# FFN gate and up by seven products of halves for half of each column group, and the FFN in five stretches

## The chip, the cores and the metric

The kernel runs on one core of a Trainium2 chip, as one program. The metric is the device time of one execution in microseconds (us), as the median of several runs. A core has five engines that run side by side and wait for each other by semaphores: TensorE (PE, matrix products; its weight loads are shown as PEld), VectorE (DVE), ScalarE (ACT), GpSimd (POOL) and SyncE (SP, which here issues all DMAs). Matmuls accumulate in PSUM, eight banks of 512 fp32 values per partition; everything else lies in SBUF.

## The reference

A decoder trunk of two layers over 256 tokens of width 2048, all in fp32. Layer A mixes by a gated position mixing beside attention to a memory, layer B by latent attention beside attention to a memory. Each layer then has a dense SwiGLU FFN with a hidden width of 5632:

```
def swiglu_ffn(h, w_gate, w_up, w_down):
    return (jax.nn.silu(h @ w_gate) * (h @ w_up)) @ w_down
...
    h = h + rms_norm(mix, norm_gains[i, 1])
    f = swiglu_ffn(rms_norm(h, norm_gains[i, 2]), ffn_w_gate[i], ffn_w_up[i], ffn_w_down[i])
    h = h + rms_norm(f, norm_gains[i, 3])
```

The change concerns `h @ w_gate` and `h @ w_up`, two products of 256 x 2048 by 2048 x 5632 per layer.

## The kernel before

**Numbers.** Every large product is done in three matmuls (`mm3`, L208 to L214): each operand is split into a rounded high half (`hi`) and the rest (`lo`), and hi x hi, hi x lo and lo x hi are added up in PSUM. ScalarE makes `hi`, VectorE makes `lo` as source minus `hi`. `wsplit` (L174 to L188) does it for 1024 weight values per partition at a time; with a gain, both operations also multiply each contraction row by its norm gain, so that the features themselves can stay unscaled. `split` (L164) does it for features.

**FFN stages.** `ffn` (L404) works in stretches of groups. A group is 512 gate and 512 up columns, and a stretch takes 3, 4 and then 4 groups (`parts`). For each group `stream` (L190) loads 1 MB of weights per DMA, two contraction tiles of 128 rows, and yields them split. `tok_major` (L223) runs 12 matmuls 512 wide on each tile: two token halves, gate and up, three matmuls. After 16 tiles the four banks hold gate and up of both token halves. ScalarE then applies Silu with the row's norm factor `r` (L427), VectorE multiplies it with up (L429), four transposes per token half turn the result into features (`turn`, L236, transposes at L240), and these are split into the pair `hp`.

After a stretch `to_tokens` multiplies `hp` with the rows of `w_down` that belong to it. The first stretch leaves its result in `Y` (L445), the second adds to it (L447), and the last runs through `residual`, which ends the layer.

**Buffers.** Weights are staged in three buffers `wst` of two tiles each, and split into a ring of four `whi` and four `wlo`. The eight PSUM banks form two sets of four, which groups take in turn; while one set is summed up, the other is read out, and its banks also take the transposes (`short`).

**Order.** The small work beside the matmuls is written as generators in a list `bg`, and `tick` advances them after each contraction tile. The framework that builds the program then sets the order of each engine's queue anew, by the order of the text and by when it expects operands to be ready; `issue_after` pins a few of them. On the chip each engine runs its queue in that order, and an instruction that waits holds up all behind it on that engine.

**Norm.** `norm_scale` (L247) computes the norm factor of each token, as a column `r_x` for token-major results, and (if `R` is given) as a row `R_x` over all partitions by one more small matmul (L268).

Of the kernel before, what the change touches and what calls it, by code (L numbers as in the profile page):

```python
# [17 lines left out]
P = 128  # L18
D = 2048
# [29 lines left out]
def trunk(ctx, tc, x, mem, positions, norm_gains, w_mem_kv, w_down, a_w_in, a_b_s, a_w_out, w_kv_a, w_uk, w_uv,  # L49
# [199 lines left out]
    def norm_scale(src, r, R):  # L249

        ss = sm.tile([P, 2, 4], F32, tag="ss", name="ss")
        for b in range(2):
            for j in range(4):
                with behind(line["act"]):
                    sumsq(src[b][:, j * 512:(j + 1) * 512], ss[:, b, j:j + 1])
                if j % 2:
                    yield
        s1 = sm.tile([P, 2], F32, tag="s2", name="s2")
        dve.tensor_reduce(out=s1, in_=ss, axis=AX.X, op=ALU.add)
        rstd(r, mean_eps(s1, 2, 1.0 / D), 2)  # L260
        if R is None:
            return
# [140 lines left out]

    def ffn(i, xp, r, gcol, gb, each, hp, need):  # L404
        parts = [(0, 3), (3, 4), (7, 4)]
        behind_group = []

        def to_features(hvs, f):

            for b in range(2):  # L410
                turn(hvs[b], hp, b, f)
                yield

        for pi, (c0, ncn) in enumerate(parts):
            for c in range(ncn):
                X = g4()
                col = (c0 + c) * 1024
                for k, wt, first, last in stream([w_gate_up[i]], [(col, 1024)], list(range(KD)), gcol):
                    tok_major(xp, k, wt, 0, 512, [X[:2], X[2:]], first, last)
                    tick()  # L420
                if pi == 0 and c == 0:
                    drain([need])
                drain(behind_group)
                hvs = []
                for b in range(2):
                    sg = tmp.tile([P, 512], F32, tag="sg", name="sg")
                    act.activation(out=sg, in_=X[2 * b], func=AF.Silu, scale=r[:, b:b + 1])  # L427
                    hv = tmp.tile([P, 512], F32, tag="hv", name="hv")
                    dve.scalar_tensor_tensor(out=hv, in0=X[2 * b + 1], scalar=r[:, b:b + 1], in1=sg,  # L429
                                             op0=ALU.mult, op1=ALU.mult)  # L430
                    hvs.append(hv)
                short["banks"] = X
                behind_group[:] = [to_features(hvs, c * 4)]
                bg.append(behind_group[0])
            ks = list(range(ncn * 4))
# [5 lines left out]
            if pi < len(parts) - 1:  # L441
                def evac(b, c, n, o):
                    yv = Y[:, b, c:c + n]
                    if pi == 0:
                        act.copy(out=yv, in_=o)  # L445
                    else:
                        dve.tensor_tensor(out=yv, in0=o, in1=yv, op=ALU.add)  # L447

                to_tokens(w_down[i], hp, ks, c0 * 4, evac, gate=gate)
            else:  # L450
                return to_tokens(w_down[i], hp, ks, c0 * 4, *residual(gb, False, each, i == 0), gate=gate)

# [35 lines left out]
    for i in range(2):  # L488
        kT = const.tile([P, 4, S], F32, name=f"mk{i}")
        vm = const.tile([P, 2, 512], F32, name=f"mv{i}")  # L490
        X = g4()
# [70 lines left out]
    with tc.tile_pool(name="mixa", bufs=1) as ma:  # L562
# [4 lines left out]
                             compare_op=ALU.is_ge, fill=0.0)  # L567
        bs = ma.tile([P, NH, P], F32, name="bs")
        sp.dma_start(out=bs, in_=a_b_s.broadcast_to([P, NH, P]))
# [142 lines left out]

    need = chain(rest, norm_scale([h[:, b, :] for b in range(2)], r_x, None))
    bg += [need, tables()]
    rest = ffn(0, xp, r_x, G_F0, gain_bcast(0, 3), turned(pair_b), pair_a, need)


    bg.append(chain(rest, norm_scale([h[:, b, :] for b in range(2)], r_x, R_x)))
    xp, mp = pair_b, pair_a
    qT = mb.tile([P, 4, S], F32, name="qTb")  # L720
    L = g4()
# [43 lines left out]
    drain([lat])  # L765
    krT = [mb.tile([P, S], F32, name=f"krT{e}") for e in range(2)]

    def rope(dst, src, n):
# [4 lines left out]
        for lo, c1, c2, op in ((0, cb, sb, ALU.subtract), (32, sb, cb, ALU.add)):  # L773
            t1 = mb.tile([P, 2, 4, 32], F32, tag="rope1", name="rope1")[:, :, :n, :]
            t2 = mb.tile([P, 2, 4, 32], F32, tag="rope2", name="rope2")[:, :, :n, :]
            dve.tensor_tensor(out=t1, in0=x1, in1=c1, op=ALU.mult)
# [116 lines left out]
    for g in lat:  # L893
        next(g)
    short["banks"] = [M[3], L[2], L[3]]
    bg[:0] = lat
# [29 lines left out]

    need = chain(rest, norm_scale([h[:, b, :] for b in range(2)], r_x, None))
    bg.append(need)
    ffn(1, xp, r_x, G_F1, gain_bcast(1, 3), store, pair_a, need)

# [41 lines left out]
```

## Time and profile before

| | |
|---|---|
| median of 3 runs | 2157.45 us (2156.25 to 2158.76) |
| profiled execution, its own time | 2159.11 us |
| its span | 2157.4 us |
| TensorE busy | 99% of the span, 10670 matmuls |
| weight loads (PEld) | 84%, beside the matmuls |
| VectorE busy | 55%, 1527 instructions |
| ScalarE busy | 47%, 1248 instructions |
| DMA | 398.71 MB, 54.9% of the 16 engines' time |

The span is the time from the first to the last instruction of one profiled execution. TensorE's durations in the rows overlap, since a matmul starts while the one before is still draining; what one costs is read from the distance between starts. In section 2 of the page the span is cut into 40 slices, and each digit is a busy share in tenths.

### The profile page before, as it was taken

Reading aid. Unit: us, or ns where it says so; the run is one execution under the profiler, and the core shown is the slowest. Engines: PE = TensorE matmul, PEld = TensorE weight load, DVE = VectorE, ACT = ScalarE, POOL = GpSimd, SP = SyncE. Lnnn points to the kernel's source line nnn. Section 1 sums busy time; section 2 is a strip of 40 time slices with the busy share of each in tenths; the row PEclk is TensorE's granted clock in tenths of the full one; section 3 lists DMA queues with packets and bytes.
Section 4 is the critical chain, followed back from the end, with each engine's and each line's share of the span. In section 5 each row is a group of like instructions: output and inputs, shape, how many; then the busy total and the mean of one; then the engine's idle time right before and its main releaser. Section 6 shows DMA issues by size and latency. Waiting matters only on the chain.

```text
span 2157.4 us, 26321 instructions
## 1 busy us (share of the span) xinstructions
PE 2134.8 (99%) x10670; PEld 1802.1 (84%) x10670; DVE 1191.9 (55%) x1527; ACT 1014.5 (47%) x1248; POOL 4.8 (0%) x11
## 2 busy tenths in 40 slices
PE   8999999999999999999999999999999999999998
PEld 7889989788888888888899998978888888888888
DVE  6556576644444454444467775664444445444456
ACT  6545445544444443444455654554444444344443
POOL 0000000000000000000000000000000000000000
PEclk9999999999999999999999999999999999999999
DMA  9655365555555555555553544555555555555554
GB/s 365 251 176 173 121 215 195 192 178 190 182 192 178 190 180 195 177 192 178 175 195 134 185 132 137 176 195 176 191 182 192 178 191 179 195 177 193 177 175 137
DMA packets 115849, 398.71 MB, mean 185 GB/s; under 512 B 7184, under 2 KB 15632, under 8 KB 114704
## 3 DMA queue, kind: packets, MB, share of 16 engines
q1 hardware_dynamic: 115728, 397.04, 54.9%
q8 instruction: 83, 1.36, 0.2%
q14 instruction: 38, 0.31, 0.0%
HBM read 394.91 MB, written 2.10 MB: 184 GB/s over the span
## 4 chain that ended last, share of the span: by engine, by line
PE 96%; DVE 3%; ACT 1%; issue 0%; DMA 0%; SPq 0%; DVEq 0%; ACTq 0%
PE bank L213 31%; PE bank L214 31%; PE bank L212 31%; PE bank L240 1%; DVE wlo L187 1%; DVE h L364 0%; PE bank L857 0%; PE bank L858 0%; PE bank L550 0%; PE bank L882 0%; ACT whi L185 0%; PE bank L604 0%; DVE hl L167 0%; PE bank L544 0%; ACT hl L166 0%
## 5 line engine op out<-in xcount | busy, mean ns | idle before, releaser
L212 PE MATMUL bank<-whi,hl 128*128 128x512 f32 (+3 forms) x2752 | 1057.7, 385 | 0.8 <-ACT hl L166 0.7
L213 PE MATMUL bank<-wlo,hl 128*128 128x512 f32 (+3 forms) x2752 | 1051.9, 382 | 1.9 <-DVE wlo L187 1.5
L214 PE MATMUL bank<-whi,hl 128*128 128x512 f32 (+3 forms) x2752 | 1051.6, 382 | 0.0
L187 DVE SCALAR_TENSOR_TENSOR wlo<-wst,gains,whi 128x1024 fp32r<-128x1024 f32 (+3 forms) x504 | 625.9, 1245 | 586.2 <-ACT whi L185 583.5
L185 ACT ACTIVATE whi<-wst,gains 128x1024 fp32r<-128x1024 f32 (+3 forms) x504 | 564.5, 1122 | 681.9 <-PE bank L214 569.6
L213 PEld LDWEIGHTS bank<-wlo,hl 128*128 128x128 f32 x2752 | 517.5, 188 | 103.4 <-DVE wlo L187 2.8
L214 PEld LDWEIGHTS bank<-whi,hl 128*128 128x128 f32 x2752 | 517.0, 188 | 104.0 <-DVE hl L167 0.4
L212 PEld LDWEIGHTS bank<-whi,hl 128*128 128x128 f32 x2752 | 517.2, 188 | 100.6 <-ACT hl L166 1.5
L181 DVE TENSOR_TENSOR wlo<-wst,whi 128x1024 fp32r<-128x1024 f32 (+1 forms) x256 | 296.1, 1157 | 313.4 <-ACT whi L179 313.3
L179 ACT CAST whi<-wst 128x1024 fp32r<-128x1024 f32 (+1 forms) x256 | 254.5, 995 | 362.6 <-PE bank L214 340.7
L212 PE MATMUL bank<-hl,whi 128*128 128x256 f32 x448 | 129.1, 288 | 6.7 <-ACT whi L185 6.7
L214 PE MATMUL bank<-hl,wlo 128*128 128x256 f32 x448 | 127.0, 284 | 1.2 <-DVE wlo L187 1.2
L213 PE MATMUL bank<-hl,whi 128*128 128x256 f32 x448 | 127.0, 284 | 0.0
L212 PEld LDWEIGHTS bank<-hl,whi 128*128 128x128 f32 x448 | 85.1, 190 | 9.9 <-ACT whi L185 6.7
L213 PEld LDWEIGHTS bank<-hl,whi 128*128 128x128 f32 x448 | 85.1, 190 | 2.7
L214 PEld LDWEIGHTS bank<-hl,wlo 128*128 128x128 f32 x448 | 84.8, 190 | 1.7 <-DVE wlo L187 1.6
L167 DVE TENSOR_TENSOR hl<-bank,hl 128x512 fp32r<-128x512 f32 (+2 forms) x97 | 55.2, 580 | 1.3 <-ACT hl L166 0.6
L166 ACT CAST hl<-bank 128x512 fp32r<-128x512 f32 (+2 forms) x97 | 46.7, 493 | 12.4 <-PE bank L240 8.7
L427 ACT ACTIVATE sg<-bank,r_x 128x512 f32<-128x512 f32 x44 | 29.7, 680 | 8.1 <-PE bank L214 8.1
L429 DVE SCALAR_TENSOR_TENSOR hv<-bank,r_x,sg 128x512 f32<-128x512 f32 x44 | 30.9, 745 | 1.4 <-ACT sg L427 1.4
L212 PE MATMUL bank<-cT,whi 128*128 128x256 f32 x96 | 28.1, 293 | 0.0
L213 PE MATMUL bank<-cT,whi 128*128 128x256 f32 x96 | 27.5, 287 | 0.0
(172 smaller groups left out, 742.4 us busy)
## 6 DMA issues: line engine op xcount, KB each, us to landing
wst<-in_w_gate_up SPq DMA_DIRECT2D x176, 1024.0 KB, 4.9
wst<-in_ffn_w_down SPq DMA_DIRECT2D x72, 1024.0 KB, 4.8
wst<-in_a_w_in SPq DMA_DIRECT2D x24, 1024.0 KB, 5.1
wst<-in_w_mem_kv SPq DMA_DIRECT2D x15, 1024.0 KB, 6.9
wst<-in_ffn_w_down SPq DMA_DIRECT2D x16, 768.0 KB, 4.3
wst<-in_a_w_out SPq DMA_DIRECT2D x8, 1024.0 KB, 4.8
wst<-in_b_w_in SPq DMA_DIRECT2D x8, 1024.0 KB, 5.0
wst<-in_b_w_out SPq DMA_DIRECT2D x8, 1024.0 KB, 5.4
```

What stands on the lines that cost most here:

```text
L166: ins = act.copy(out=hi, in_=src)
L167: dve.tensor_tensor(out=lo, in0=src, in1=hi.bitcast(F32), op=ALU.subtract)
L179: act.copy(out=hi[:, :n], in_=src)
L181: dve.tensor_tensor(out=lo[:, :n], in0=src, in1=hi[:, :n].bitcast(F32), op=ALU.subtract)
L185: act.activation(out=hi[:, :n], in_=src, func=AF.Copy, scale=g)
L187: dve.scalar_tensor_tensor(out=lo[:, :n], in0=src, scalar=g, in1=hi[:, :n].bitcast(F32), op0=ALU.mult, op1=ALU.subtract)
L212: pe.matmul(out=o, lhsT=a[0], rhs=b[0], start=start, stop=False, **kw)
L213: pe.matmul(out=o, lhsT=a[0], rhs=b[1], start=False, stop=False, **kw)
L214: line["pe"] = pe.matmul(out=o, lhsT=a[1], rhs=b[0], start=False, stop=stop, **kw).ins
L240: pe.transpose(out=pt[:, q * P:(q + 1) * P], in_=src[:, q * P:(q + 1) * P], identity=ident)
L427: act.activation(out=sg, in_=X[2 * b], func=AF.Silu, scale=r[:, b:b + 1])
L429: dve.scalar_tensor_tensor(out=hv, in0=X[2 * b + 1], scalar=r[:, b:b + 1], in1=sg, op0=ALU.mult, op1=ALU.mult)
```

## The change

The last four stretches of each FFN (five in all, with 2, 2, 2, 2 and 3 groups) treat the two halves of a group differently; the first stretch stays as it was. The weights lie in memory with 256 gate and 256 up columns in turn, so that a half group is 512 columns.

- Half of each group is done as a product of 2 x 2 blocks: two token halves by two halves of the contraction on the left, two halves of the contraction by gate and up on the right. Instead of eight block products seven are summed up, each with sums of blocks as operands. The sums of the feature blocks are made once per layer (`normalise`, kept in `sx` and `sz`), the sums of the weight blocks for each quarter of the contraction (`seven_step`), and the results are put together from the seven sums in PSUM (`seven_hidden`). These matmuls are 256 wide.
- The other half of the group runs beside it as before (`plain_step`), 512 wide, into two banks; a quarter of the one and a quarter of the other alternate.
- The sums need features that carry gain and norm factor already, so `normalise` multiplies them in place by gain and `R_x` and splits them again; its first two quarters run in the second group of the first stretch, the others in the first down stretch. `norm_scale` makes `R_x` for the FFN too.
- Room for it: `sx` shares the buffers of the first memory keys and of layer A's position biases, `sz` is the upper half of `hp`, layer B's small tiles share a buffer with `sx`, and the gain row of the last residual is loaded at the last down stretch instead of at the start of the FFN.

The core of the diff (`plain_step`, `hidden` and the renamed rooms are cut):

```diff
-        parts = [(0, 3), (3, 4), (7, 4)]
+        parts = [(0, 2), (2, 2), (4, 2), (6, 2), (8, 3)]
+        sx = [const.tile([P, 8, S], F32R, tag=("mkv0", "sx")[e], name=f"sx{e}") for e in range(2)]
+        sz = [t[:, 8:, :] for t in hp]
+        halves = [t.rearrange("p (h k) t -> p h k t", h=2) for t in xp]
...
+        def normalise(g):
...
+            own = [t[:, :, 2 * g:2 * g + 2, :] for t in halves]
+            dve.tensor_tensor(out=xr, in0=own[0].bitcast(F32), in1=own[1].bitcast(F32), op=ALU.add)
+            yield
+            for e in range(2):
+                for j in range(2):
+                    k = gcol + 8 * e + 2 * g + j
+                    dve.scalar_tensor_tensor(out=xr[:, e, j, :], in0=xr[:, e, j, :], scalar=gains[:, k:k + 1], in1=R,
+                                             op0=ALU.mult, op1=ALU.mult)
+            yield
+            split(*own, xr)
...
+        def stage(col, g):
+            st = wtile().rearrange("p (h k n) -> p h k n", h=2, k=2)
+            rows = w_gate_up[i].rearrange("(h k p) n -> p h k n", h=2, p=P)
+            for e in range(2):
+                sp.dma_start(out=st[:, e], in_=rows[:, e, 2 * g:2 * g + 2, col:col + 512])
+            return st
...
+        def seven_step(col, g, X):
+            st = stage(col, g)
+            room = tmp.tile([P, D], F32, tag="gb", name="ws", bufs=2)
+            t13, t24 = room[:, :1024], room[:, 1024:]
+            b11, b21, b22 = st[:, 0, :, :S], st[:, 1, :, :S], st[:, 1, :, S:]
+            sums = room.rearrange("p (s k n) -> p s k n", s=4, k=2)
+
+            def products(wt, *what):
+                for at, (a, k, b, o, start) in enumerate(what):
+                    for j in range(2):
+                        c = slice((2 * at + j) * S, (2 * at + j + 1) * S)
+                        mm3(o, [t[:, k + 2 * g + j, b * P:(b + 1) * P] for t in a], [t[:, c] for t in wt],
+                            start and g == 0 and j == 0, g == 3 and j == 1)
+                tick()
+
+            wt = parts_of_sum(st[:, :, :, :S])
+            dve.tensor_tensor(out=sums[:, 0:2], in0=st[:, :, :, S:], in1=st[:, 0].rearrange("p k (x n) -> p x k n", x=2),
+                              op=ALU.add)
+            products(wt, (xp, 0, 0, X[0][:, :S], True), (xp, 8, 0, X[0][:, S:], False))
+            wt = parts_of_sum(t13)
+            dve.tensor_tensor(out=sums[:, 2], in0=sums[:, 1], in1=b11, op=ALU.add)
+            products(wt, (sz, 0, 0, X[1][:, S:], True), (sx, 0, 0, X[1][:, :S], False))
+            dve.tensor_tensor(out=sums[:, 3], in0=sums[:, 2], in1=b21, op=ALU.add)
+            wt = parts_of_sum(t24)
+            products(wt, (sz, 0, 1, X[3][:, :S], True), (xp, 8, 1, X[2][:, :S], True))
+            wt = parts_of_sum(b22, 512)
+            products(wt, (sx, 0, 1, X[2][:, S:], False))
+
+        def seven_hidden(X, f):
+            m1, m2, m5, m6 = X[0][:, :S], X[0][:, S:], X[1][:, S:], X[3][:, :S]
+            v = tmp.tile([P, 512], F32, tag="lat", name="v", bufs=2)
+            act.copy(out=v[:, :S], in_=m1)
+            dve.tensor_tensor(out=v[:, S:], in0=m6, in1=v[:, :S], op=ALU.add)
+            u = tmp.tile([P, 512], F32, tag="lat", name="u", bufs=2)
+            dve.tensor_tensor(out=u.rearrange("p (x n) -> p x n", x=2), in0=X[1].rearrange("p (x n) -> p x n", x=2),
+                              in1=v[:, S:].rearrange("p (o n) -> p o n", o=1).broadcast_to([P, 2, S]), op=ALU.add)
+            dve.tensor_tensor(out=m1, in0=m2, in1=v[:, :S], op=ALU.add)
+            sg = tmp.tile([P, 512], F32, tag="sg", name="sg")
+            act.activation(out=sg[:, :S], in_=m1, func=AF.Silu)
+            dve.tensor_tensor(out=X[2], in0=X[2], in1=u, op=ALU.add)
+            act.activation(out=sg[:, S:], in_=X[2][:, :S], func=AF.Silu)
+            dve.tensor_tensor(out=m5, in0=m5, in1=u[:, :S], op=ALU.add)
+            hv = tmp.tile([P, 512], F32, tag="hv", name="hv")
+            for b, o in enumerate((X[2][:, S:], m5)):
+                c = slice(b * S, (b + 1) * S)
+                dve.scalar_tensor_tensor(out=hv[:, c], in0=o, scalar=-1.0, in1=sg[:, c], op0=ALU.mult, op1=ALU.mult)
+            behind_group.append(to_features(hv, f))
...
+                seven, other = g4(), g4()
+                short["banks"] = other[2:]
+                for c in range(ncn):
+                    col = (c0 + c) * 1024
+                    for g in range(4):
+                        seven_step(col, g, seven)
+                        if g == 3:
+                            behind_done()
+                            seven_hidden(seven, c * 4)
+                        plain_step(col + 512, g, other[:2])
+                    behind_done()
+                    hidden(other[:2], c * 4 + 2, False)
...
-    need = chain(rest, norm_scale([h[:, b, :] for b in range(2)], r_x, None))
+    need = chain(rest, norm_scale([h[:, b, :] for b in range(2)], r_x, R_x))
...
-    gate_up = [a[n].reshape(2, D, DFF // 512, 512) for n in ("ffn_w_gate", "ffn_w_up")]
+    gate_up = [a[n].reshape(2, D, DFF // S, S) for n in ("ffn_w_gate", "ffn_w_up")]
```

## Rows read from the trace of the kernel before

**Rows 1.** Page, section 1: busy time, share and instructions; section 2: TensorE's granted clock.

```profile
PE 2134.8 (99%) x10670; PEld 1802.1 (84%) x10670; DVE 1191.9 (55%) x1527; ACT 1014.5 (47%) x1248; POOL 4.8 (0%) x11
...
PEclk9999999999999999999999999999999999999999
```

**Rows 2.** Page, section 4: the chain that ended last, shares by engine.

```profile
PE 96%; DVE 3%; ACT 1%; issue 0%; DMA 0%; SPq 0%; DVEq 0%; ACTq 0%
```

**Rows 3.** Timeline of TensorE in a gate and up group: start, duration, engine, line, operation.

```profile
600.10 0.40 PE L213 MATMUL bank<-wlo,hl 128*128 128x512 f32 x1
...
603.83 0.40 PE L214 MATMUL bank<-whi,hl 128*128 128x512 f32 x1
```

**Rows 4.** Timeline of TensorE where 256-wide matmuls follow each other, two places.

```profile
60.24 0.28 PE L212 MATMUL bank<-hl,whi 128*128 128x256 f32 x1
...
61.56 0.28 PE L214 MATMUL bank<-hl,wlo 128*128 128x256 f32 x1
...
2137.76 0.28 PE L213 MATMUL bank<-wlo,hl 128*128 128x256 f32 x1
...
2139.90 0.28 PE L213 MATMUL bank<-wlo,hl 128*128 128x256 f32 x1
```

**Rows 5.** Timeline of ScalarE: the first gating of two groups that follow each other.

```profile
621.42 0.67 ACT L427 ACTIVATE sg<-bank,r_x 128x512 f32<-128x512 f32 x1
...
667.09 0.67 ACT L427 ACTIVATE sg<-bank,r_x 128x512 f32<-128x512 f32 x1
```

**Rows 6.** Timeline of TensorE around four transposes of the gated result.

```profile
625.77 0.60 PE L240 MATMUL bank<-ident,hv 128*128 128x128 f32 x4
...
626.43 0.39 PE L213 MATMUL bank<-wlo,hl 128*128 128x512 f32 x1
```

**Rows 7.** Groups by line and form: shapes, count, busy us, mean ns, idle before.

```profile
L181 DVE TENSOR_TENSOR wlo<-wst,whi 128x1024 fp32r<-128x1024 f32 x192 | 235.0, 1224 | 247.8 <-ACT whi L179 247.8
L179 ACT CAST whi<-wst 128x1024 fp32r<-128x1024 f32 x192 | 201.1, 1048 | 282.3 <-PE bank L214 260.5 <-issue 17.9 <-DVE turn L695 2.1
...
L167 DVE TENSOR_TENSOR hl<-bank,hl 128x512 fp32r<-128x512 f32 x65 | 43.7, 683 | 0.8 <-ACT hl L166 0.6
...
L167 DVE TENSOR_TENSOR hl<-bank,hl 128x256 fp32r<-128x256 f32 x20 | 8.0, 418 | 0.2
...
L608 DVE SCALAR_TENSOR_TENSOR Y<-bank,gains,bs 128x256 f32<-128x256 f32 x12 | 5.2, 477 | 3.8 <-PE bank L604 3.8
```

**Rows 8.** Timeline of VectorE where operations stand queued behind each other.

```profile
804.34 1.22 DVE L181 TENSOR_TENSOR wlo<-wst,whi 128x1024 fp32r<-128x1024 f32 x1
805.47 1.88 DVE L447 TENSOR_TENSOR Y<-bank,Y 128x512 f32<-128x512 f32 x3
807.27 1.21 DVE L181 TENSOR_TENSOR wlo<-wst,whi 128x1024 fp32r<-128x1024 f32 x1
...
1220.75 0.42 DVE L776 TENSOR_TENSOR rope<-bank,cos 128x256 f32<-128x256 f32 x1
1221.09 0.15 DVE L123 TENSOR_TENSOR rt<-ry 128x2 f32<-128x2 f32 x1
```

**Rows 9.** Windows behind the first layer's end: busy us, clock, DMA share, GB/s.

```profile
1130.00:1140.00 10.00, 10.00 (x75) 9.27 (x74) 9.81 (x16) 9.80 (x22) 0.00 (x0) 1.00 0.01 2
1140.00:1150.00 10.00, 10.00 (x67) 9.12 (x66) 9.36 (x21) 5.35 (x9) 0.00 (x0) 1.00 0.89 316
```

**Rows 10.** The same view, last down columns, loaded in runs of 1 KB.

```profile
2123.00:2142.00 19.00, 19.00 (x126) 18.98 (x125) 12.32 (x19) 8.97 (x15) 0.00 (x0) 1.00 0.32 107
```

**Rows 11.** Waits: engine and line, waited for; us in all, times, longest.

```profile
ACT whi L185 <- PE bank L214: 569.6, 366, 2.5
```

**Rows 12.** Timeline of VectorE at the end of a stretch's last group.

```profile
508.58 1.23 DVE L181 TENSOR_TENSOR wlo<-wst,whi 128x1024 fp32r<-128x1024 f32 x1 [1.57 <-ACT whi L179]
...
509.72 1.41 DVE L429 SCALAR_TENSOR_TENSOR hv<-bank,r_x,sg 128x512 f32<-128x512 f32 x2
```

**Rows 13.** DMA issues: queue, count, size of each, median us to landing.

```profile
wst<-in_w_gate_up SPq DMA_DIRECT2D x176, 1024.0 KB, 4.9
```

More of the change, by code (lines that the diff above doesn't have):

```diff
@@ L402, in residual, with ffn @@
         return evac, finish
-    def ffn(i, xp, r, gcol, gb, each, hp, need):
-        parts = [(0, 3), (3, 4), (7, 4)]
+    def ffn(i, xp, r, R, gcol, each, hp, need):
+        parts = [(0, 2), (2, 2), (4, 2), (6, 2), (8, 3)]
         behind_group = []
-        def to_features(hvs, f):
-            for b in range(2):
-                turn(hvs[b], hp, b, f)
-                yield
-        for pi, (c0, ncn) in enumerate(parts):
[L415 to L434, printed above, removed]
@@ new lines, in plain_step @@
+        def plain_step(col, g, banks):
+            st = stage(col, g)
+            for e in range(2):
+                wt = wsplit(st[:, e].rearrange("p k n -> p (k n)"), 1024)
+                for j in range(2):
+                    tok_major(xp, 8 * e + 2 * g + j, wt, 512 * j, 512, [[o] for o in banks],
+                              g == 0 and e == 0 and j == 0, g == 3 and e == 1 and j == 1)
+                    if j == 0:
+                        tick()
+                tick()
+        early = list(range(4)) + list(range(8, 12)) + list(range(4, 8)) + list(range(12, 16))
@@ new lines, in ffn, with scaling @@
+        ready = [0]
+        def scaling():
+            for g in range(4):
+                while g >= ready[0]:
+                    yield
+                yield from normalise(g)
+        scaled = scaling()
+        for pi, (c0, ncn) in enumerate(parts):
+            if pi == 0:
+                for c in range(ncn):
+                    X = g4()
+                    for at, (k, wt, first, last) in enumerate(
+                            stream([w_gate_up[i]], [(c * 1024, 1024)], early if c else list(range(KD)), gcol)):
+                        tok_major(xp, k, wt, 0, 512, [X[:2], X[2:]], first, last)
+                        if c == 1 and at == 7:
+                            ready[0] = 2
+                            bg.append(scaled)
+                        tick()
+                    if c == 0:
+                        drain([need])
+                    behind_done()
+                    for j in range(2):
+                        hidden([X[j], X[2 + j]], c * 4 + 2 * j, True)
+                    short["banks"] = X
+                ready[0] = 4
+            else:
+                seven, other = g4(), g4()
+                short["banks"] = other[2:]
+                for c in range(ncn):
+                    col = (c0 + c) * 1024
+                    for g in range(4):
+                        seven_step(col, g, seven)
[3 more added lines that the diff above has]
+                        plain_step(col + 512, g, other[:2])
+                    behind_done()
+                    hidden(other[:2], c * 4 + 2, False)
```

78 lines of the change are left out of this document (64 added, 14 removed).

## The prediction

> **What bounds the kernel now.** I read the page first. TensorE is busy 2134.8 of 2157.4 us at full granted clock in every slice, VectorE 1191.9 and ScalarE 1014.5 [rows 1]; the chain of waits lies on TensorE for 96% [rows 2]. Then the waits: what the splitters wait for is TensorE itself, ScalarE's first half of a split 569.6 us in 366 waits for a used buffer to come free [rows 11]. So the ring of four split buffers runs full, and each us of matmul removed inside the FFN is a us of the end, as long as nothing else comes to bound there. Last the timelines, for prices. The profiled execution took 2159.1 us (span 2157.4); the median of the runs shown is 2157.45, so 1.7 us come off at the end.
>
> **Matmuls removed and added.** In the plain half of a group 512-wide matmuls follow each other every 0.2331 us (600.10 to 603.83, 16 steps) [rows 3]. A 256-wide one with a new weight load each time takes 0.1189 us (2137.76 to 2139.90, 18 steps) and 0.120 in the other place read (60.24 to 61.56, 11 steps) [rows 4]. A group has 192 wide ones: 44.8 us, and two batches of four transposes, each 0.43 us beyond a plain step (625.77 to 626.43 less 0.233) [rows 6]: 45.6 us. The trace's own group is 667.09 - 621.42 = 45.7 [rows 5], so TensorE waits for nothing in it. Seven products of 8 contraction tiles at 3 matmuls are 168 narrow ones, 20.0 us, in place of 96 wide ones, 22.4: a group goes to 43.2 us. Nine groups of eleven in each of two layers are changed: 18 x 2.42 = 43.5 us. With 0.120 it is 40; were the narrow one just half the wide one, 50. Transposes stay at eight a group, matmuls of the down product keep their number.
>
> **VectorE's work.** This is the term that decides, so both ends. One quarter of a group (a seven-step and a plain step) now has six operations of 1024 (five low halves of splits, one sum) and three of 512 (half a split, two sums). By full row lengths (1.224 and 0.683 [rows 7]) that is 9.39 us, and 37.6 a group. The recombination adds three of 256 from PSUM (0.418), two of 512 and two scaled ones of 256 (0.477): 3.6; the plain half's gating 0.84, the two splits of the turned features 1.37. Together 43.4 us a group against TensorE's 43.2. Queued operations overlap, though: starts lie 1.13 us apart behind one of 1024 (804.34 to 805.47) and 0.60 behind one of 512 (805.47 to 807.27 for three), 0.34 behind one of 256 [rows 8]. With these, and 0.39 for the scaled ones (their row less the same 0.08), the quarter is 8.58, the group 34.3 + 3.0 + 0.7 + 1.2 = 39.2 us, 91% of TensorE's. Three of the recombination's operations write PSUM (256, 512 and 256), which no row before does; nearest are the reads from it. If each costs as much again the group rises by 1.5, to 40.7; if they cost as in SBUF, by nothing. I take the overlapped price, nearest to rows of a full queue. The rows show that VectorE can run so: 9.81 and 9.36 busy of 10 us in two stretches behind the layer's end while TensorE lost nothing [rows 9].
>
> The Trainium skill says otherwise in VectorE: DVE Perf Modes, The DRAIN you can't avoid: each operation is followed by a flush, and the next starts only when the pipe is empty. By that the group's sum is the 43.4 of full lengths, VectorE is the bound by a hair, and the gain falls to what the second rival has. The trace does not bear it out for operations that don't depend on each other: each row starts about 0.09 us before the one ahead of it ends [rows 8].
>
> **What of it lies on the path.** The average leaves 4.0 us of VectorE free per group; the spread does not. At the last quarter it has 8.6 + 3.0 + 0.6 = 12.2 us against 10.6 of TensorE, in the next quarter 9.9. The surplus of 1.6 must come from the lead of up to three prepared sets, which a seven-step uses up in 1.43 us a set and a plain one in 2.8. The tightest set is the plain step's first: its buffers come free when the first pair of products ends, 1.43 us into the quarter, ScalarE needs 1.05 [rows 7], VectorE 1.22, so it is ready at some 3.8, wanted at 5.2; one 1.13 us operation in front still fits, two don't. Loss per group between 0 and 1.6 us. Four of the nine ends have a down stretch behind them, where VectorE has one split of 1.22 per 2.8 us and catches up, so 5/9 of 1.6 is 0.9 with no lead used at all and 0 with all of it; I take 0.6: 18 x 0.6 = 11 us.
>
> **The rest.** Rescaling the features in place: per quarter about 7.5 us of VectorE (two of 1024, eight of 256, two of 512), half of it in the second group, where VectorE is half idle, half in the first down stretch: hidden; uncovered, the last quarter is wanted only 32 us into the second stretch. Two more down stretches per layer: 16 more sums of 0.68 beside 45 us of matmuls each; 0 on the path, at most one sum of 0.68 per new stretch where it stands in front of a split. The row factors need one 256-wide matmul more per layer, which may wait for VectorE in TensorE's queue: between 0.1 and 1 us each, taken as 0.5, 1 us in all. The gain row of the last residual moves from the layer's start to the SP queue just ahead of the last down weights, and waits for one of two buffers that the sums use: behind it stand the next weights, 4.9 us a load [rows 13]; three loads and three split sets are ahead, so 0, at most 3 per layer. Loads by runs of 2 KB in place of 4: 2.1 MB per 10.6 us is 198 GB/s; runs of 1 KB had 107 GB/s at 0.32 of the engines [rows 10], and 316 at 0.89 was reached with long ones [rows 9], both some 340 at full share: no cost. ScalarE: 5.5 x 1.05 per quarter, 23 of 43 us, and some 3 more: no bound. Shared rooms and the other bank order in the attention layer: within 1 us either way, taken as 0.
>
> Sum: 2159.1 - 43.5 + 11 + 1 = 2127.6 in the profiled execution, 2126 for the median.
>
> **Rivals.**
> *No stall.* VectorE's lead covers every group end: 2115. For: the rows of full load without a gap [rows 9]. Against: those are 20 us, here it is 87 and more at a time. It is the near end of the likeliest case.
> *VectorE becomes the engine that bounds.* Full lengths, or dear PSUM writes: 43.4 a group, and idle moments of VectorE now count: one wait for a whole half of ScalarE's (1.05) with its hand-overs a group, 1.5 more by estimate, 44.9. Left of the gain is 0.8 x 18 = 14 us: 2144, range 2137 to 2153. For: the sums need each other's results in turn, which the overlapped rows do not. Against: that holds for two short ones a quarter; the rest is free to overlap as in [rows 8].
> *TensorE held at each group's end: slower.* If VectorE's queue has the recombination ahead of the plain step's first low half, TensorE ends the seventh product, then waits for the add of 512 (0.68), 0.42, two gatings (0.95) behind a ScalarE activation, and 1.22 for the split: 3.3 us, some 3.6 with the hand-overs. 18 x 3.6 = 65, net 21 slower: 2180. It decides from 2.4 us per group on. For: VectorE's queue is in order, and in program order it is so. Against: the order is not that of the program. At a group's end now a low half of the next stage (508.58) runs ahead of the gating (509.72), though the text has the gating first [rows 12].
> *The products don't pay.* Narrow matmuls cost too much: even at 22.4 / 168 = 0.1333 us each. Both rows are well below; nearly excluded.
>
> **How the numbers follow.** Within 0.2% (4.3 us) a measurement can't tell a change. Likeliest case 0.60, its own range 2115 to 2137 (0 to 1.2 us lost per group); better than that 0.04 (wide matmuls dearer, or mixer rooms a gain); VectorE as the bound 0.18, of which 0.03 ends within 0.2%; held at the group ends 0.14, of which 0.03 within 0.2%; anything else, a queue that I costed at nothing, 0.04, shared between same and slower. Faster 0.60 + 0.04 + 0.15 = 0.79, same 0.07, slower 0.14. The range 2112 to 2152 leaves out the slower cases and the tail of the third.
>
> **What would show it.** Right: narrow matmuls at 0.119 us, a changed group at 43 to 44.5 us, VectorE above 85% in the gate and up stretches, TensorE still near 98% busy, idle before the low halves' matmuls under 15 us. Second rival: VectorE above 96% there, TensorE's idle put down to low halves all through the group. Third: idle in one piece after the seventh product, or at the transposes. Wrong altogether: narrow matmuls above 0.13, granted clock below 1.00 in these stretches, or idle put down to loads.

## The result and the profile after

The changed kernel takes 2119.5 us in the median of 4 runs (2117.61 to 2121.68), against 2156.85 us for the kernel before beside it (2153.65 to 2158.76): a ratio of 0.983 with a 95% interval of 0.981 to 0.985. The forecast was 2126 us. The profiled execution took 2121.68 us (span 2120.0, granted clock 0.998), 37.4 us less than the one before.

The page first: busy time of each engine; the busy tenths of VectorE and TensorE's granted clock in 40 slices; the shares of the chain of waits.

```profile
PE 2094.3 (99%) x11922; PEld 1835.1 (87%) x11922; DVE 1568.0 (74%) x2151; ACT 1119.4 (53%) x1478; POOL 4.1 (0%) x11
...
DVE  6556755976868878689767775597686877868966
...
PEclk9999999999999999999999999999999999999999
...
PE 91%; DVE 5%; DMA 2%; ACT 1%; issue 1%; SPq 0%; DVEq 0%; ACTq 0%
```

Against [rows 1] TensorE is busy 40.5 us less, with 1252 more (narrower) matmuls, and VectorE 376 us more. The chain still lies on TensorE; VectorE's share of it has gone from 3 to 5%, and loads come in with 2% [rows 2].

The prices, from TensorE's timeline in one changed group (start, duration, engine, line, operation): the first wide matmul of a plain step, the first narrow one of the seven-step behind it, and the first wide one behind that.

```profile
560.96 0.39 PE L212 MATMUL bank<-whi,hl 128*128 128x512 f32 x1
...
566.53 0.28 PE L212 MATMUL bank<-whi,hl 128*128 128x256 f32 x1
...
571.52 0.39 PE L212 MATMUL bank<-whi,hl 128*128 128x512 f32 x1
```

A plain step has 24 wide matmuls in 5.57 us, 0.232 each, and a seven-step 42 narrow ones in 4.99 us, 0.119 each. A quarter of a group is 10.56 us; four of them and the transposes are 43.1 us, where a group was 45.6.

VectorE's groups by line and form (shapes, count, busy us, mean ns, idle before). The last two write PSUM, which no row of before did:

```profile
L181 DVE TENSOR_TENSOR wlo<-wst,whi 128x1024 fp32r<-128x1024 f32 x342 | 415.4, 1221 | 181.2 <-ACT whi L179 179.9
...
L504 DVE TENSOR_TENSOR ws<-wst 128x1024 f32<-128x1024 f32 x72 | 88.0, 1223 | 26.1 <-DMA wst<-in_w_gate_up 25.7
...
L528 DVE TENSOR_TENSOR bank<-bank,u 128x512 f32<-128x512 f32 x18 | 12.4, 690 | 0.0
...
L525 DVE TENSOR_TENSOR bank<-bank,v 128x256 f32<-128x256 f32 x18 | 7.7, 429 | 3.6 <-ACT v L520 3.6
```

What TensorE waited for (us in all, times, longest): the low halves of the split cost little, and the transposes behind the gating almost nothing.

```profile
PE bank L213 <- DVE wlo L181: 1.9, 2, 1.3
...
PE bank L418 <- DVE hv L534: 0.4, 2, 0.2
```

Windows of three changed groups (about the two of the first changed stretch, and the second of the last one), and then two at the first layer's end (us; busy us of TensorE, its weight loads, VectorE, ScalarE, GpSimd, each with its count; granted clock; DMA share; GB/s):

```profile
510.00:553.00 43.00, 42.93 (x267) 38.35 (x266) 35.42 (x40) 26.02 (x31) 0.00 (x0) 1.00 0.56 178
553.53:596.60 43.07, 42.86 (x272) 38.36 (x271) 38.05 (x45) 25.02 (x31) 0.00 (x0) 1.00 0.60 199
...
950.70:993.80 43.10, 43.10 (x273) 38.91 (x272) 39.48 (x47) 25.56 (x31) 0.00 (x0) 1.00 0.58 194
...
1104.00:1108.00 4.00, 2.33 (x18) 1.90 (x17) 3.68 (x12) 3.28 (x5) 0.00 (x0) 1.00 0.39 109
1108.00:1112.00 4.00, 3.86 (x11) 2.36 (x12) 2.86 (x12) 0.48 (x2) 0.00 (x0) 0.57 0.40 162
```

In the first changed group VectorE is busy 35.4 of 43 us, 82%, in the next 38.1 of 43.1, 88%, and in the third 39.5 of 43.1, 92%, the highest of the 18; TensorE is busy for 42.9 us or more in each.

**Where the 37.4 us come from.** Fixed points in both traces divide them: the first FFN is 19.1 us shorter (758.0 to 738.9 us, between the first operation of VectorE that adds a result to `h` in the residual before it and in the one after it), the second 19.6, and the mixers and the tail together 1.3 longer. By prices the 18 changed groups are worth 18 x 2.5 = 45. Gaps between starts, beyond the spacing just read, add up to 3.1 us in the first FFN and 1.5 in the second, where before had none. That leaves 45 - 4.6 - 38.7 = 1.7 us inside the FFNs, not located.

Outside the FFNs, the first one begins 1.5 us later (366.75 for 365.24 us). In eight of the experiments below, whose text is the same up to there, it begins between 364.8 and 366.4 us, so most of this is scatter of single executions. The mixer behind the first layer's end takes 267.0 us for 266.6, and the tail is 0.7 shorter. In that mixer, the window at 1108 shows a mean granted clock of 0.57, so for most of its 4 us the lower level, 1.2 GHz; TensorE had been busy 2.33 of the 4 us before. Other executions show what this costs: in five of the experiments the clock stays at 1.00 through that place, and the mixer takes 266.0 us; in three it falls there as here, and the mixer takes 267.1 to 267.5. So the fall is worth some 1.0 to 1.5 us.

The largest single stall of TensorE in the first FFN, 1.3 us at 670, has its cause on VectorE's timeline:

```profile
663.55 1.23 DVE L167 TENSOR_TENSOR wlo<-ws,whi 128x1024 fp32r<-128x1024 f32 x1 [1.15 <-ACT whi L166]
...
667.33 1.23 DVE L504 TENSOR_TENSOR ws<-wst 128x1024 f32<-128x1024 f32 x1 [2.55 <-DMA wst<-in_w_gate_up]
...
669.07 0.69 DVE L508 TENSOR_TENSOR ws<-ws,wst 128x512 f32<-128x512 f32 x1
669.79 0.69 DVE L510 TENSOR_TENSOR ws<-ws,wst 128x512 f32<-128x512 f32 x1
```

VectorE stood 2.55 us before a sum whose weights had not landed. It waits like this 35 times, 25.7 us in all, and this is the one place where it costs TensorE over a us. The last two rows are sums of which the second needs the first one's result: they start 0.72 us apart, so they don't overlap, while independent operations of this length start 0.60 apart. All 16 such pairs that follow each other directly lie some 0.72 us apart.

### The profile page after: what moved, and what is told of

Its sections match the earlier page's. It is cut to its first block, busy times and chain, and to the rows that moved or that the text cites. A ratio compares the mean times of both kernels' runs of the same rounds, so it can differ in the third digit from the quotient of the medians.

```text
span 2120.0 us, 30041 instructions
## 1 busy us (share of the span) xinstructions
PE 2094.3 (99%) x11922; PEld 1835.1 (87%) x11922; DVE 1568.0 (74%) x2151; ACT 1119.4 (53%) x1478; POOL 4.1 (0%) x11
## 4 chain that ended last, share of the span: by engine, by line
PE 91%; DVE 5%; DMA 2%; ACT 1%; issue 1%; SPq 0%; DVEq 0%; ACTq 0%
PE bank L214 29%; PE bank L213 29%; PE bank L212 29%; DMA wst<-in_w_gate_up 2%; PE bank L418 1%; DVE wlo L181 1%; DVE wlo L187 1%; DVE h L362 1%; PE bank L240 0%; PE bank L1016 0%; PE bank L1017 0%; DVE ws L504 0%; PE bank L707 0%; PE bank L1041 0%; DVE wlo L167 0%
## 5 line engine op out<-in xcount | busy, mean ns | idle before, releaser
L212 PE MATMUL bank<-whi,hl 128*128 128x512 f32 (+3 forms) x2880 | 1030.8, 359 | 0.9 <-ACT hl L166 0.7
L214 PE MATMUL bank<-whi,hl 128*128 128x512 f32 (+3 forms) x2880 | 1025.5, 356 | 0.0
L181 DVE TENSOR_TENSOR wlo<-wst,whi 128x1024 fp32r<-128x1024 f32 (+1 forms) x398 | 468.8, 1183 | 237.5 <-ACT whi L179 236.2
L214 PEld LDWEIGHTS bank<-whi,hl 128*128 128x128 f32 x2880 | 542.3, 188 | 77.6 <-DVE hl L167 0.5
L212 PEld LDWEIGHTS bank<-whi,hl 128*128 128x128 f32 x2880 | 542.5, 188 | 76.2 <-ACT hl L166 1.9
L179 ACT CAST whi<-wst 128x1024 fp32r<-128x1024 f32 (+1 forms) x398 | 405.0, 1020 | 381.2 <-PE bank L214 346.3
L187 DVE SCALAR_TENSOR_TENSOR wlo<-wst,gains,whi 128x1024 fp32r<-128x1024 f32 (+3 forms) x216 | 255.7, 1193 | 131.0 <-ACT whi L185 128.1
L185 ACT ACTIVATE whi<-wst,gains 128x1024 fp32r<-128x1024 f32 (+3 forms) x216 | 232.2, 1080 | 216.7 <-PE bank L214 131.2
L166 ACT CAST whi<-ws 128x1024 fp32r<-128x1024 f32 x144 | 151.1, 1049 | 159.0 <-PE bank L214 81.0
L167 DVE TENSOR_TENSOR wlo<-ws,whi 128x1024 fp32r<-128x1024 f32 x144 | 175.6, 1220 | 57.0 <-ACT whi L166 56.8
L166 ACT CAST whi<-wst 128x1024 fp32r<-128x1024 f32 (+1 forms) x144 | 120.3, 835 | 108.1 <-PE bank L214 107.3
L167 DVE TENSOR_TENSOR wlo<-wst,whi 128x1024 fp32r<-128x1024 f32 (+1 forms) x144 | 137.0, 951 | 22.0 <-ACT whi L166 22.0
L504 DVE TENSOR_TENSOR ws<-wst 128x1024 f32<-128x1024 f32 x72 | 88.0, 1223 | 26.1 <-DMA wst<-in_w_gate_up 25.7
L213 PE MATMUL bank<-wlo,sx 128*128 128x256 f32 x288 | 81.2, 282 | 0.0
```

The source lines that it names most:

```text
L166: ins = act.copy(out=hi, in_=src)
L167: dve.tensor_tensor(out=lo, in0=src, in1=hi.bitcast(F32), op=ALU.subtract)
L179: act.copy(out=hi[:, :n], in_=src)
L181: dve.tensor_tensor(out=lo[:, :n], in0=src, in1=hi[:, :n].bitcast(F32), op=ALU.subtract)
L185: act.activation(out=hi[:, :n], in_=src, func=AF.Copy, scale=g)
L187: dve.scalar_tensor_tensor(out=lo[:, :n], in0=src, scalar=g, in1=hi[:, :n].bitcast(F32), op0=ALU.mult, op1=ALU.subtract)
```

## The experiments

**The theory**: the gain is the seventh less multiplying, 2.5 us a group; TensorE stays the bound, because VectorE's queued operations overlap, so that it has about 4 us to spare per group; and the lead of four prepared buffers carries the group's end. **The rivals**: something else in the change gives the gain (five stretches, the new memory order); VectorE has no time to spare; the group's end holds TensorE up.

**Both halves plain.** All else of the change is kept.

```diff
-                        seven_step(col, g, seven)
+                        plain_step(col, g, seven[:2])
...
-                            seven_hidden(seven, c * 4)
+                            hidden(seven[:2], c * 4, False)
```

> Five stretches, rescaled features and the new loads stay, but both halves of each group are summed by eight wide products, 96 matmuls of 512 each. Theory (the gain is TensorE's removed matmul time, the rest of the change is hidden): within 0.2% of the kernel before, 2153 to 2161 us. Rival (part of the gain comes from the rest, as from splits without a gain): more than 0.2% below before.

2160.59 us, ratio 1.0018 (1.0009 to 1.0027). The rest of the change gains nothing; by the medians it costs 3.9 us (1.9 to 5.8). In the profiled executions it is 0.8 us, and the first FFN takes 757.8 us, as before (758.0), so no cost shows in there.

**Eight products in place of seven**, by the same narrow matmuls, without any sum:

```diff
-                        seven_step(col, g, seven)
+                        eight_step(col, g, seven)
...
+        def eight_step(col, g, X):
+            st = stage(col, g)
+            for e in range(2):
+                wt = wsplit(st[:, e].rearrange("p k n -> p (k n)"), 1024)
+                for j in range(2):
+                    tok_major(xp, 8 * e + 2 * g + j, wt, 512 * j, S, [X[0:2], X[2:4]],
...
```

> As e1_plain5, but one half of each group by eight products 256 wide into four banks: 192 narrow matmuls of 0.1188 in place of 96 wide ones of 0.232, no sums of weights and no recombination. Theory: 0.5 us more a group than plain, 18 x 0.5 = 9 above e1, about 2166, and 18 x 2.85 = 51 less 5 of stalls, so 46, above the changed kernel. Rival (narrow matmuls cost nothing extra, what the changed kernel lost is all waiting): equal to e1.

2164.94 us, ratio 1.0038 (1.0023 to 1.0052): 4.35 above the plain version, 45.4 above the change. Cutting the matmuls in two costs 4.35 us (9 expected); leaving one product in eight away then gives 45, net of what the sums cost. By the spacing, 24 narrow matmuls a group are 18 x 24 x 0.119 = 51 us; less the 4.6 us of gaps that is 47. The gain comes from that product alone.

**Two idle sums on VectorE** in each seven-step, 512 wide, of operands that are always there:

```diff
+            for _ in range(2):
+                idle = tmp.tile([P, 512], F32, tag="junk", name="idle", bufs=1)
+                dve.tensor_tensor(out=idle, in0=h[:, 0, :512], in1=h[:, 1, :512], op=ALU.add)
```

> The changed kernel with two idle sums of 512 more on VectorE in each seven-step: 1.2 us a quarter, 4.8 a group, so 39.2 + 4.8 = 44.0 against TensorE's 43.1. Theory (overlapped prices, VectorE at 91% before): now just over the bound, 16 to 45 us above the changed kernel's 2119.5, 2136 to 2165. Rival (full row lengths are the price, VectorE was at 43.4 already): 48.8 a group, at least 18 x 5.5 = 100 more, 2220. Rival (VectorE has far more room than either): within 5 us of 2119.5.

2120.11 us, ratio 0.9835 (0.9818 to 0.9851): no cost, against 16 to 45 us expected. The dose was not spread as meant. The order built for VectorE's queue had moved the sums forward: of the first layer's 72, 42 run before 497 us and 26 between 500 and 588. But this made a stretch as full as could be wished. Windows of it (columns as above):

```profile
500.00:520.00 20.00, 20.00 (x109) 17.14 (x108) 19.83 (x26) 11.57 (x14) 0.00 (x0) 1.00 0.46 159
...
540.00:560.00 20.00, 19.94 (x129) 17.65 (x128) 19.74 (x28) 11.99 (x18) 0.00 (x0) 1.00 0.44 155
560.00:580.00 20.00, 19.81 (x122) 17.46 (x121) 19.34 (x23) 10.42 (x12) 0.00 (x0) 1.00 0.60 211
580.00:600.00 20.00, 20.00 (x118) 17.26 (x117) 19.53 (x27) 12.45 (x17) 0.00 (x0) 1.00 0.73 239
```

In the five windows from 500 to 600 us, nearly all of it changed groups, VectorE is busy 19.3 to 19.8 of 20 us, and TensorE is idle for a quarter of a us in all.

**The same sums on the staged weights**, which holds them in their step: two of them (4.8 us a group at the overlapped 0.60), and four (9.6).

```diff
+            for e in range(2):    # four: range(4)
+                idle = tmp.tile([P, 512], F32, tag="junk", name="idle", bufs=1)
+                dve.tensor_tensor(out=idle.rearrange("p (k n) -> p k n", k=2), in0=b21, in1=b22, op=ALU.add)
```

> As e3_dve2, where 68 of the 72 first layer sums that were to load VectorE ran before or in the first stretch; here the two idle sums of 512 read the step's own staged weights, so that they can't run elsewhere: 4.8 us a group, 39.2 + 4.8 = 44.0 against TensorE's 43.1. Theory (overlapped prices are right): VectorE over the bound by 0.9 us a group, made up for in part in the down stretches: 10 to 35 us above the changed kernel, 2130 to 2155. Rival (VectorE still has room, prices too high): within 5 us of 2119.5. Rival (full lengths): above 2200.

> As e5_dve2w with four idle sums: 9.6 us a group, 48.8 against 43.1. Theory: VectorE bounds, 18 x 5.7 = 103 less what the down stretches take over (a lead of some 5 us per stretch, 8 stretches, 40), 2180 to 2225. Rival (room left): below 2150.

2133.87 us, ratio 0.9890 (0.9874 to 0.9906), and 2181.87, ratio 1.0112 (1.0096 to 1.0128): 14.4 and 62.4 us above the change. Of the first 86 us of added work 14 arrive at the end, of the second 86 us 48. Both lie in their theory's range, the second at its near end. A straight line through both meets zero at 3.35 us a group: that is about what VectorE has to spare (an estimate: the true curve bends, and the second dose loses some time to the clock too). In the second one the waits of TensorE (first two rows) are for sums' splits, and some stretches (window) lose clock as well:

```profile
PE bank L213 <- DVE wlo L167: 18.7, 33, 0.9
PE bank L212 <- ACT whi L166: 12.8, 10, 2.0
...
560.00:580.00 20.00, 19.13 (x109) 16.11 (x108) 19.94 (x23) 7.92 (x9) 0.00 (x0) 1.00 0.61 211
...
820.00:840.00 20.00, 17.40 (x93) 15.33 (x92) 19.49 (x27) 9.45 (x14) 0.00 (x0) 0.83 0.45 155
```

So with VectorE as the bound the gain can turn into a loss; the change keeps clear of it by some 3.4 us in 43.

**The three weight sums on GpSimd**, to relieve VectorE:

```diff
-            dve.tensor_tensor(out=sums[:, 0:2], in0=st[:, :, :, S:], in1=st[:, 0].rearrange("p k (x n) -> p x k n", x=2),
+            pool_e.tensor_tensor(out=sums[:, 0:2], in0=st[:, :, :, S:], in1=st[:, 0].rearrange("p k (x n) -> p x k n", x=2),
...
-            dve.tensor_tensor(out=sums[:, 3], in0=sums[:, 2], in1=b21, op=ALU.add)
+            pool_e.tensor_tensor(out=sums[:, 3], in0=sums[:, 2], in1=b21, op=ALU.add)
```

> The changed kernel with the three sums of weight blocks on GpSimd instead of VectorE, which takes 2.33 us a quarter from VectorE. Theory: only the 4.6 us of stalls that TensorE still has can go, 2115 to 2120. Rival (VectorE's load hides more, as the bound of a stretch): 2110 or less. Rival (GpSimd is slow at it, at 1.4 ns an element 2.9 us a quarter, and the sums come late or hold VectorE up): above 2124.

2162.35 us, ratio 1.0025 (1.0016 to 1.0034), 43 slower than the change. Three operations in each of 72 seven-steps have left VectorE, and it is busy longer (1588 us). By form its splits have grown from a mean of 1221 ns:

```profile
L181 DVE TENSOR_TENSOR wlo<-wst,whi 128x1024 fp32r<-128x1024 f32 x342 | 530.6, 1562 | 231.8 <-ACT whi L179 231.4
```

GpSimd's and VectorE's timelines side by side show how:

```profile
544.77 2.41 POOL L504 TENSOR_TENSOR ws<-wst 128x1024 f32<-128x1024 f32 x1 [3.93 <-DMA wst<-in_w_gate_up]
547.26 2.16 POOL L508 TENSOR_TENSOR ws<-ws,wst 128x512 f32<-128x512 f32 x1
```

```profile
545.95 2.32 DVE L181 TENSOR_TENSOR wlo<-wst,whi 128x1024 fp32r<-128x1024 f32 x1 [0.52 <-ACT whi L179]
548.19 0.41 DVE L521 TENSOR_TENSOR v<-bank,v 128x256 f32<-128x256 f32 x1
548.52 1.98 DVE L181 TENSOR_TENSOR wlo<-wst,whi 128x1024 fp32r<-128x1024 f32 x1
```

GpSimd's first sum ends at 547.18, and the split that started during it ends 1.09 us later, at 548.27; GpSimd's second sum, issued at 547.26, ends 1.15 us after that, at 549.42; the next split ends at 550.50, 1.08 us behind it. They take turns, while the operation that reads PSUM (0.41) keeps its price. So it goes through the whole execution: VectorE's 197 operations of 1024 that overlap one of these sums take 2.11 us in the mean, the other 548 take 1.24, and in each of the 387 overlapping pairs whose operands all lie in SBUF the one that ends later does so at least 1.08 us (VectorE, 1024 values) or 0.54 (512) behind the other, GpSimd's 2.26 or 1.13. By this GpSimd needs some 4.5 us a quarter for the three sums, by estimate, where 2.9 was expected. The Trainium skill has this rule in SBUF — State Buffer, Who interferes with whom: the two engines share a pair of ports under an exclusive lock. These rows agree.

What TensorE waits for then is the gated result at the transposes, at the end of the groups; in the change such waits were 0.4 us in all:

```profile
PE bank L418 <- DVE hv L534: 18.7, 11, 1.7
PE bank L418 <- DVE hv L434: 12.2, 8, 1.6
```

**The plain step's first split pinned behind the recombination**, which is the third rival made true:

```diff
+                pin[0] = dve.scalar_tensor_tensor(out=hv[:, c], in0=o, scalar=-1.0, in1=sg[:, c], op0=ALU.mult,
+                                                  op1=ALU.mult).ins
...
+                with behind(pin[0] if g == 3 and e == 0 else None):
+                    wt = wsplit(st[:, e].rearrange("p k n -> p (k n)"), 1024)
```

> The changed kernel with the low half of the plain step's first set in the last quarter pinned behind the recombination's last gating on VectorE's queue, as the program's text has it. Theory (the order set at build time is what avoids the third rival's stall): TensorE waits 3.3 to 3.6 us at each of 18 group ends, 59 to 65 above the changed kernel, 2178 to 2185. Rival (the chain is done before TensorE needs the set): within 5 us of 2119.5.

2172.75 us, ratio 1.0072 (1.0056 to 1.0088), 53 above the change: 3.0 us a group, where 3.3 to 3.6 was expected. TensorE's waits and its timeline at one group's end:

```profile
PE bank L418 <- DVE hv L534: 20.6, 18, 1.3
...
PE bank L213 <- DVE wlo L181: 8.4, 20, 1.4
```

```profile
550.53 0.88 PE L418 MATMUL bank<-ident,hv 128*128 128x128 f32 x4 [1.31 <-DVE hv L534]
...
551.99 0.57 PE L213 MATMUL bank<-wlo,hl 128*128 128x512 f32 x1 [0.46 <-DVE wlo L181]
...
552.79 0.63 PE L213 MATMUL bank<-wlo,hl 128*128 128x512 f32 x1
553.22 0.63 PE L214 MATMUL bank<-whi,hl 128*128 128x512 f32 x1
...
555.74 0.39 PE L214 MATMUL bank<-whi,hl 128*128 128x512 f32 x1
555.97 0.39 PE L212 MATMUL bank<-whi,hl 128*128 128x512 f32 x1
```

Two windows behind that (columns as above):

```profile
552.50:555.00 2.50, 2.50 (x8) 1.92 (x7) 2.50 (x4) 0.00 (x0) 0.00 (x0) 0.50 0.22 44
556.00:558.00 2.00, 2.00 (x10) 1.65 (x9) 0.71 (x1) 1.05 (x1) 0.00 (x0) 1.00 0.74 285
```

At this group's end the two waits, 1.8 us, are followed by a granted clock of 0.50, that is 1.2 GHz, with wide matmuls 0.43 us apart, and from 555.7 on by 1.00 and 0.23 again: here the stall is paid once as a wait and once more as clock. This holds for 6 of the 18 group ends. At the others the same waits (1.30 and 0.47 us at 690) or shorter ones are followed by wide matmuls 0.23 us apart, at the full clock. Between starts the two waits cost 2.3 us at the ten ends that have a group behind them and 1.7 at the eight that have a down stretch, 36 us in all, and the clock some 10 more, by the spacing; the other 7 are not located.

In the change itself VectorE's queue at the same place reads otherwise:

```profile
547.92 1.22 DVE L181 TENSOR_TENSOR wlo<-wst,whi 128x1024 fp32r<-128x1024 f32 x1
549.06 0.42 DVE L521 TENSOR_TENSOR v<-bank,v 128x256 f32<-128x256 f32 x1
549.39 1.21 DVE L181 TENSOR_TENSOR wlo<-wst,whi 128x1024 fp32r<-128x1024 f32 x1
550.52 0.68 DVE L523 TENSOR_TENSOR u<-bank,v 128x512 f32<-128x512 f32 x1
551.12 1.21 DVE L167 TENSOR_TENSOR wlo<-wst,whi 128x1024 fp32r<-128x1024 f32 x1
552.26 0.69 DVE L528 TENSOR_TENSOR bank<-bank,u 128x512 f32<-128x512 f32 x1
```

Splits of the next steps (1.2 us) stand between the operations of the recombination. The order of the queue is what saves the 53 us.

**Three split buffers in place of four**, in the changed kernel (in `wsplit` and in `parts_of_sum`) and, as a control, in the kernel before (in `wsplit` alone, which makes all its sets):

```diff
-        hi = wpool.tile([P, 1024], F32R, tag="whi", name="whi", bufs=4)
-        lo = wpool.tile([P, 1024], F32R, tag="wlo", name="wlo", bufs=4)
+        hi = wpool.tile([P, 1024], F32R, tag="whi", name="whi", bufs=3)
+        lo = wpool.tile([P, 1024], F32R, tag="wlo", name="wlo", bufs=3)
```

> The changed kernel with three split buffers in place of four, each way. Theory (the lead of prepared sets covers the uneven load of VectorE): with one set less the steps after the narrow ones come late by 0 to 1 us a quarter, 72 quarters, 10 to 70 us slower, 2130 to 2190, TensorE's waits on low halves. Rival (VectorE simply has enough time, the lead doesn't matter): within 5 us of 2119.5.

> The kernel before with three split buffers in place of four, each way: the control of e7_ring3, which lost 84 us. Theory (the fourth buffer is needed by the narrow, uneven steps of the change): in the FFN of before a set is used up in 2.8 us and made in 2.4, so nothing is lost there; the mixers may lose some 10 us, 2157 to 2170. Rival (three buffers are too few for any of it): 40 us or more, above 2195.

The changed kernel: 2203.56 us, ratio 1.0215 (1.0196 to 1.0233), 84 above the change with four, more than expected. The kernel before: 2172.07, ratio 1.0068 (1.0053 to 1.0083), 14 above. TensorE's waits and one window of the changed kernel with three:

```profile
PE bank L212 <- ACT whi L166: 22.9, 10, 2.3
PE bank L213 <- DVE wlo L167: 12.2, 14, 2.1
...
560.00:580.00 20.00, 16.88 (x104) 15.37 (x103) 14.88 (x19) 9.30 (x12) 0.00 (x0) 0.91 0.36 121
```

The waits are for the seven-steps' splits, and they don't lie all through the groups: all ten for a high half (2.3 us each) and ten of the fourteen for a low half behind it stand in the first seven-step of a group that follows directly on another one. There are ten such places, the five of nine group ends of each layer that have no down stretch behind them. There the recombination, the gatings and the splits of the gated features stand in VectorE's queue together with the next splits: around the first of them it works almost without a pause from 551.6 to 568 us, while in the 20 us of the window it is busy for only 14.9. What is missing is room to prepare ahead, not VectorE's time on the average. The two FFNs are 29.3 and 40.6 us longer than with four buffers, the rest of the execution 10.5. Some 19 of these us are clock, by the spacing where it is granted at 0.50. In the control the FFNs are as long as before to within 1 us; its 14 us lie at the layers' ends and in the mixers. So 70 of the 84 us are the changed groups', and they are lost where the work of VectorE bunches up.

**Half the loads.** Each step loads the first half of its weights and uses it twice:

```diff
-            for e in range(2):
-                sp.dma_start(out=st[:, e], in_=rows[:, e, 2 * g:2 * g + 2, col:col + 512])
-            return st
+            sp.dma_start(out=st[:, 0], in_=rows[:, 0, 2 * g:2 * g + 2, col:col + 512])
+            return st[:, 0:1].broadcast_to([P, 2, 2, 512])
```

> The changed kernel with half of the weights of each seven-step and plain step left out (the second half of the contraction is given the first half's weights, so the result is not the reference's): 512 KB in place of 1 MB per step. Theory (of the 4.6 us of stalls that TensorE has left in the FFNs, two of the waits for low halves hang on loads that came late, the rest on the recombination): 1 to 4 us less than the changed kernel's 2119.5. Rival (loads by 2 KB runs cost more than the trace shows): more than 5 us less. Rival (loads are no matter at all): within 1 us.

2115.37 us, ratio 0.9804 (0.9788 to 0.9821), 4.1 less than the change. The gaps of TensorE in the gate and up stretches shrink from 4.6 us in both layers to about 0.5. So nearly all of the 4.6 us hang on the loads, as the stall at 670 does. By which path each of them does is not shown: VectorE's waits for loads are longer in sum here (40.9 us against 25.7), only TensorE no longer feels them. Against the kernel before, each as timed beside it, this kernel gains 42.4 us and the change 37.4, so the effect is 4 to 5 us, at the border between the theory's 1 to 4 and the first rival's "more than 5". The edit halves the bytes and the number of loads at once, so it doesn't tell whether the 2 KB runs or the sheer amount cost this.

## Why the prediction was right

The mechanism held: TensorE stays the bound, and the seventh less multiplying is the gain. The number came out as near as it did in part by luck, since errors in the smaller terms cancel: the group ends were priced some 10 us too dear, the loads and the rest some 6 too cheap.

- **Matmuls: 43.5 us by prediction, 45 measured.** The narrow price came as read from [rows 4] (0.119); a group takes 43.1 us where 43.2 was forecast, against 45.6. The 45.4 us between eight and seven narrow products are another sum: 51 us of matmuls less the stalls. That the narrow form is dearer than half a wide one was in the price; it shows as 4.35 us, half of the 9 expected.
- **VectorE's overlapped price: confirmed.** Taken as 39.2 us a group, 91% of TensorE's, against the 43.4 of full row lengths. Measured are 35.4 to 39.5 us, the low end in the first group of an FFN's changed ones. In its queue independent operations of 1024, 512 and 256 start 1.13, 0.60 and 0.33 us apart (the rows from 547.92 on). And had VectorE been the bound already, the first dose would have cost about what the second did, 48 us; it cost 14.4. Spare time comes out at some 3.4 us, forecast 4.0. The PSUM writes, bounded between nothing and 1.5 us a group, came at the cheap end: 690 and 429 ns, as the reads do [rows 7].
- **The flush between VectorE's operations.** Here the prediction read only half of the section. The Trainium skill, VectorE: DVE Perf Modes, The DRAIN you can't avoid, says that the next operation doesn't start until the pipe is empty, and then that one that is not held starts earlier. The rows agree with the second: independent operations, queued without a wait, start some 0.08 us before the row ahead ends. A sum that needs the one before it starts 0.03 us behind that one's end (669.07 and 669.79).
- **Stalls at the group ends: 11 us by prediction, at most 4.6 measured**, and hardly there: with the loads halved, 0.5 of the 4.6 is left. I took 0.6 us a group, between nothing and 1.6, from a surplus of 1.6 us that the lead would only partly cover. The lead covers almost all of it. The picture behind the term is right: with three sets in place of four the stalls appear, nearly all at the five of nine ends per layer that have no down stretch behind them. The rival *No stall*, at 2115, was thus closer than its place at the near end suggests; the kernel lies between the two.
- **Loads** I had at no cost; they cost some 4 us, nearly all of the stalls that are left. Idle time put down to loads was to be a sign of being wrong altogether; at 4 us of 37 it is not that, only a term left out.
- **The rest: 1 us by prediction, some 3 measured** (1.7 inside the FFNs and 1.3 outside), 3.9 by the medians of the version with both halves plain. I had the mixers at nothing. What shows there is the fall of the clock behind the first layer's end, 1.0 to 1.5 us, and scatter.
- **The sum**: -43.5 + 11 + 1 = -31.5 predicted, -45 + 4.6 + 3.0 = -37.4 measured in the profiled execution.
- **Third rival**: its price, 3.6 us a group, was near the 3.0 that pinning it costs, and its result, 2180, near 2172.75. What the price is made of differs: it was to be one wait for a chain that ends in the split, and it is a wait at the transposes, a shorter one for the split, and at a third of the ends a fall of the clock. The argument against the rival, that the built order puts splits ahead [rows 12], is what VectorE's timeline shows. **Second rival**: not reached, but the dose of 9.6 us shows that it exists and ends slower than before.
- ScalarE, at 26 of 43 us, is no bound, as forecast.

## What to carry to other kernels

Sums that replace a product pay as long as the engine that makes them has time to spare in the stretch where they run: price its queue by distances between starts, not by row lengths, and add what operations lose that need the one before them. Keep as many prepared buffers as the spot needs where that engine's work bunches up, not as the average needs (here four, against three: 84 us). Where an in-order queue holds both short urgent work and preparation for the next step, its order can cost as much as its load: 53 us for a single pin, 62 for the larger dose of idle work. Moving work to another engine is a gain only if the two don't shut each other out; read the row lengths of what stayed behind.

## What the runs showed of the hardware

- A VectorE operation with two SBUF inputs and a GpSimd sum of SBUF operands ran in turns here, never side by side: VectorE's splits of 1024 went from a mean of 1221 to 1562 ns, and its busy time rose though three sums a step had left it.
- VectorE's operations that read and write PSUM cost what those do that only read it: 690 ns for 512 values per partition, 429 for 256.
- A queue on VectorE that is 98% busy (19.6 of 20 us in the mean) cost TensorE a quarter of a us in 100.
- Independent operations of VectorE that stand queued start 0.08 us before the row ahead ends; a 512-wide sum that needs the result of the one before it starts 0.03 us after it (0.72 us apart in place of 0.60).
- Two short waits of TensorE, 1.31 and 0.46 us within 2 us, stand ahead of a stretch at a granted clock of 0.50 (0.43 us between wide matmuls in place of 0.23) at 6 of 18 group ends; at the other 12 the same waits or shorter ones are followed by the full clock.
